# Latent attention's query and key tiles filled straight from the bank, with a new order of the work

## The chip, the cores and the metric

One core of a Trainium2 chip runs the whole kernel. The metric is device time in microseconds (us) for one execution. The engines are TensorE (PE; its weight loads are PEld), VectorE (DVE), ScalarE (ACT), GpSimd (POOL) and SyncE (SP). Transfers are issued by SP, POOL and ACT, each with its own queue. Matmuls read SBUF tiles (`s`, `raw`, `wh`, `wl`) and write PSUM banks (`b`).

## The reference

Two layers run over 256 latent tokens and 256 context tokens of 1024 columns, in float32. Each layer has three attention branches on one projection, then a gated merge, and a squared-ReLU MLP. The branch that matters here is latent attention (`ml`): eight heads whose queries and keys are 64 plain columns and 32 rotated ones; the rotated key is shared by all heads.

```python
q_nope, q_rope = ml_q[..., :MLA_NOPE], ml_q[..., MLA_NOPE:]      # 64 and 32 per head
k_nope = (c_kv @ w_uk).reshape(b, n, MLA_HEADS, MLA_NOPE)
k_rope = ml_kr[:, :, None, :]
...
ml_q = jnp.concatenate([q_nope, q_rope], axis=-1)
ml_k = jnp.concatenate([k_nope, jnp.broadcast_to(k_rope, (b, n, MLA_HEADS, MLA_ROPE))], axis=-1)
...
yc = sdpa_blocks(pl['ml_q'][:, :, :, None, :], mk_all, mv_all, sc_m)
```

Layer 0 computes queries for latent and context tokens (512), layer 1 for the latent ones only (256). Keys always cover 512 tokens.

## The kernel before

Most matmuls are done in three passes: each operand is split into a high part (ScalarE rounds it) and a low part (VectorE subtracts), and `mm3` (L762 to L764) adds high by high, high by low and low by high. `hilo` (L804 to L812) makes such a split of a PSUM bank: ScalarE at L808 or, with a scale, L811; VectorE at L809 or L812. Weights come by SP's queue (L681) and are split at L699 (ScalarE) and L700 (VectorE).

The instructions of each engine stand in one fixed order. A planner in Python makes it before the kernel is built: a list of work items for each layer, written by hand in `SEQ`, gives the order in which items are started, and the planner plays them on modelled engines. In `SEQ`, `c0` to `c7` are the eight chunks of the first norm's modulation (each reads two weight tiles and ends in the L835 and L845 matmuls), `q`, `k`, `v` are neighbourhood attention's projections, `rope` the rotated columns, `l0` to `l3` latent attention's head pairs, `attn` starts the attention units, `g`, `o` and `w` are gates, output projections and modulation weights. A word such as `more4`, `raw1` or `less` changes how much is in flight.

For each pair of heads, `it_ml` computes a bank of 128 rows of plain query columns (64 rows for each head) and a bank of keys, and forks `ml_evac` on each. `ml_evac` takes two tiles, `s0` and `s1`, of 128 rows with a high and a low half:

- `hilo`, called at L1403, splits all 128 rows of the bank into `s0`, one ScalarE and one VectorE operation.
- L1405, a transfer on POOL's queue, copies rows 64 to 127 of `s0` (the second head) to rows 0 to 63 of `s1`.
- L1407, a transfer, puts the second head's 32 rotated rows into rows 64 to 95 of `s1`.
- L1409, a transfer, puts the first head's 32 rotated rows into rows 64 to 95 of `s0`. These rows are what L1405 reads, so L1409 waits until L1405 has landed.

`scores` then runs `mm3` on 96 rows of both tiles (L762, with the form 96*128). Eight pairs in two layers, queries and keys, make 16 calls of `ml_evac`.

Of the kernel before, what the change touches and what calls it, by code (L numbers as in the profile page):

```python
# [10 lines left out]
F32 = mybir.dt.float32  # L11
F32R = mybir.dt.float32r
AF = mybir.ActivationFunctionType
ALU = mybir.AluOpType
# [23 lines left out]
ROWS = (slice(0, 64), slice(64, 128))  # L38
# [27 lines left out]

BR = {"N": NA, "L": ML, "G": GA}
SEQ = (
# [7 lines left out]
)  # L76


# [183 lines left out]
SL_W, SL_E, SL_G = 0.5, 10.0, 13.0  # L262
# [247 lines left out]
def a_(n):  # L510

    return 0.07 + n * 0.00085


def v_(n):
    return 0.07 + n * 0.00104
# [28 lines left out]
class Prog:  # L545
# [852 lines left out]

    def ml_evac(self, l, key, bank, m, scale, rope, mem):

        nc = self.nc
        s0, s1 = self.take(mem), self.take(mem)
        yield from self.hilo(s0.ap[:, 0, :m], s0.ap[:, 1, :m], bank.ap[:, :m], m, scale, SL_E)  # L1403
        self.unbank(bank)
        yield ("pool", 1.2, lambda: nc.gpsimd.dma_start(s1.ap[0:64, :, :m], s0.ap[64:128, :, :m]))  # L1405
        yield from self.wait("qr", l)
        yield ("pool", 1.2, lambda: nc.gpsimd.dma_start(s1.ap[64:96, :, :m], rope(1)))  # L1407
        yield ("sleep", 2.5)
        yield ("pool", 1.2, lambda: nc.gpsimd.dma_start(s0.ap[64:96, :, :m], rope(0)))  # L1409
        yield ("sleep", 3.0)  # L1410
        self.qr_leaf.done()
        self.qr_leaf.done()
        self.qk[key] = [s0, s1]
        self.set(*key)


# [97 lines left out]
    def scores(self, l, br, p, s):  # L1514

        mm = self.nc.tensor.matmul
        if br == ML:
            q, k = (self.qk[(n, l, p)][s].ap[0:96] for n in ("mlq", "mlk"))
            return lambda out, i, j: self.mm3(out, (q[:, 0, i], q[:, 1, i]), (k[:, 0, j], k[:, 1, j]), True, True)
        kq, kk = self.unit_needs(l, br, p)[0]  # L1520
        q, (k, kl) = self.stacked[kq][s], self.stacked[kk]

        def make(out, i, j):
            mm(out, q[:, i], k[s][:, j], start=True, stop=False)  # L1524
            mm(out, q[:, i], kl[s][:, j], start=False, stop=True)  # L1525
        return make
# [645 lines left out]
```

## Time and profile before

| what | value |
| --- | --- |
| device time, median of 3 runs | 1448.34 us (1448.06 to 1448.86) |
| the profiled execution's own time | 1452.61 us |
| its span, first to last instruction | 1450.8 us (1.8 us lie around it) |
| mean granted TensorE clock | 0.991 |
| busy: PE, PEld | 1418.5 us (98%), 1290.5 us (89%) |
| busy: DVE, ACT, POOL | 1081.8 us (75%), 746.6 us (51%), 34.7 us (2%) |
| chain that ended last, by engine | PE 86%, DVE 6%, DMA 4%, ACT 2% |
| transfers | 210.91 MB, mean 145 GB/s |

All times below are those of the profiled execution, counted from the start of its span. The granted clock is in shares of full speed. An engine's idle time matters where the work that ends last waits for it; PE is on that chain for most of the span.

### The profile page before, as it was taken

The numbers are of one execution on the slowest core, as the hardware profiler recorded it, in microseconds if no ns is written. First come the engines' busy times: TensorE is split into PE (matmuls) and PEld (weight loads), VectorE is DVE, ScalarE is ACT, GpSimd is POOL, SyncE is SP. The second block draws the span as 40 slices with busy tenths as digits, with TensorE's granted clock in tenths as the row PEclk, the third lists the DMA queues.
The fourth block names the chain that finished last, engine by engine and source line by source line (L and its number), as shares of the span: only waits on it lengthen the run. The fifth ranks groups of instructions, "written<-read, shape, count | busy, mean of one in ns | idle before, by whom it ended". The sixth has DMA issues, their size and how long they took to land.

```text
span 1450.8 us, 23974 instructions
## 1 busy us (share of the span) xinstructions
PE 1418.5 (98%) x9294; PEld 1290.5 (89%) x9294; DVE 1081.8 (75%) x2251; ACT 746.6 (51%) x1359; POOL 34.7 (2%) x74
## 2 busy tenths in 40 slices
PE   5999999999999999999999999999999999999997
PEld 3799889988888899888888889999998999899997
DVE  6638887859986989888866547758888987766665
ACT  4528876446852344323233244348776874645543
POOL 0000110000000000000000000000111000000000
PEclk9999999999999999999999999999999999999999
DMA  8511433342225544455655424335465436455551
GB/s 324 195 41 56 111 101 90 105 152 78 86 104 189 174 145 132 153 194 180 199 199 193 149 98 141 131 99 160 127 176 144 134 105 219 155 180 188 175 189 45
DMA packets 61779, 210.91 MB, mean 145 GB/s; under 512 B 7392, under 2 KB 9440, under 8 KB 61664
## 3 DMA queue, kind: packets, MB, share of 16 engines
q1 hardware_dynamic: 56448, 197.94, 41.0%
q0 software_dynamic: 4352, 10.49, 3.2%
q8 instruction: 73, 1.20, 0.3%
q10 hardware_dynamic: 864, 0.93, 0.2%
q14 instruction: 42, 0.34, 0.1%
HBM read 200.95 MB, written 1.05 MB: 139 GB/s over the span
## 4 chain that ended last, share of the span: by engine, by line
PE 86%; DVE 6%; DMA 4%; ACT 2%; issue 1%; POOL 0%; ACTq 0%; SPq 0%; DVEq 0%; POOLq 0%
PE b L763 25%; PE b L762 25%; PE b L764 25%; PE b L1696 3%; DMA raw<-in_wts_dram 3%; PE b L1731 2%; PE b L1730 2%; DVE wl L700 1%; PE b L1524 1%; PE b L1525 1%; DMA s<-s 1%; DVE s L905 1%; DVE s L1044 1%; DMA s<-in_wts_dram 1%; PE b L1700 1%
## 5 line engine op out<-in xcount | busy, mean ns | idle before, releaser
L762 PE MATMUL b<-s,wh 128*128 128x256 f32 (+1 forms) x1664 | 566.5, 340 | 1.2 <-ACT s L1047 1.1
L763 PE MATMUL b<-s,wh 128*128 128x256 f32 (+1 forms) x1664 | 561.4, 337 | 0.9 <-DVE s L1905 0.3
L764 PE MATMUL b<-s,wl 128*128 128x256 f32 (+1 forms) x1664 | 559.8, 336 | 0.0
L699 ACT CAST wh<-raw 128x1024 fp32r<-128x1024 f32 (+3 forms) x184 | 188.4, 1027 | 341.8 <-PE b L763 290.1
L762 PEld LDWEIGHTS b<-s,wh 128*128 128x128 f32 x1664 | 317.7, 191 | 34.0 <-ACT s L1047 1.4
L763 PEld LDWEIGHTS b<-s,wh 128*128 128x128 f32 x1664 | 317.8, 191 | 33.3 <-DVE s L1048 1.7
L764 PEld LDWEIGHTS b<-s,wl 128*128 128x128 f32 x1664 | 317.4, 191 | 32.5
L700 DVE TENSOR_TENSOR wl<-raw,wh 128x1024 fp32r<-128x1024 f32 (+3 forms) x184 | 218.8, 1191 | 103.9 <-ACT wh L699 100.1
L905 DVE CUSTOM_DVE_ANT_0 s<-raw,s 128x512 f32<-128x512 f32 x248 | 170.6, 688 | 35.1 <-DMA raw<-in_wts_dram 30.8
L762 PE MATMUL b<-s,s 128*128 128x256 f32 (+4 forms) x568 | 169.5, 298 | 3.1 <-DMA s<-s 3.1
L763 PE MATMUL b<-s,s 128*128 128x256 f32 (+4 forms) x568 | 167.8, 295 | 0.0
L764 PE MATMUL b<-s,s 128*128 128x256 f32 (+4 forms) x568 | 167.5, 295 | 0.0
L762 PEld LDWEIGHTS b<-s,s 128*128 128x128 f32 (+1 forms) x568 | 109.0, 192 | 4.8 <-issue 3.3
L764 PEld LDWEIGHTS b<-s,s 128*128 128x128 f32 (+1 forms) x568 | 109.0, 192 | 2.5
L763 PEld LDWEIGHTS b<-s,s 128*128 128x128 f32 (+1 forms) x568 | 109.2, 192 | 1.4
L809 DVE TENSOR_TENSOR s<-b,s 128x512 fp32r<-128x512 f32 (+3 forms) x151 | 100.1, 670 | 13.1 <-ACT s L808 12.1
L762 PE MATMUL b<-wh,s 128*128 128x256 f32 (+1 forms) x360 | 104.0, 289 | 0.0
L764 PE MATMUL b<-wh,s 128*128 128x256 f32 (+1 forms) x360 | 102.1, 284 | 0.0
L763 PE MATMUL b<-wl,s 128*128 128x256 f32 (+1 forms) x360 | 102.1, 284 | 0.0
L1860 DVE SCALAR_TENSOR_TENSOR s<-b,mod,s 128x256 f32<-128x256 f32 x120 | 55.5, 480 | 60.6 <-PE b L764 60.4
L808 ACT CAST s<-b 128x512 fp32r<-128x512 f32 (+2 forms) x151 | 85.0, 577 | 22.1 <-PE b L764 9.1
L699 ACT CAST wh<-s 128x1024 fp32r<-128x1024 f32 x45 | 47.2, 1049 | 67.9 <-PE b L763 59.0
(157 smaller groups left out, 1892.7 us busy)
## 6 DMA issues: line engine op xcount, KB each, us to landing
raw<-in_wts_dram SPq DMA_DIRECT2D x299, 512.0 KB, 3.5
s<-in_wts_dram SPq DMA_DIRECT2D x61, 512.0 KB, 3.6
s<-in_xT_dram SPq DMA_DIRECT2D x16, 256.0 KB, 6.2
s<-s POOLq DMA_DIRECT2D x28, 128.0 KB, 4.2
s<-in_bias_dram POOLq DMA_DIRECT2D x16, 192.0 KB, 2.7
s<-s POOLq DMA_DIRECT2D x12, 256.0 KB, 3.7
raw<-in_wts_dram SPq DMA_DIRECT2D x4, 384.0 KB, 3.0
raw<-in_wts_dram SPq DMA_DIRECT2D x3, 432.0 KB, 3.8
```

What stands on the lines that cost most here:

```text
L699: yield from self.act(n, lambda: nc.scalar.copy(hi[:, :n], r[0][:, :n]), SL_W)
L700: yield from self.dve(n, lambda: nc.vector.tensor_tensor(lo[:, :n], r[0][:, :n], hi[:, :n].bitcast(F32), ALU.subtract), SL_W)
L762: mm(out, a[0], b[0], start=start, stop=False)
L763: mm(out, a[0], b[1], start=False, stop=False)
L764: mm(out, a[1], b[0], start=False, stop=stop)
L808: yield from self.act(n, lambda: nc.scalar.copy(hi, src), slack)
L809: yield from self.dve(n, lambda: nc.vector.tensor_tensor(lo, src, hi.bitcast(F32), ALU.subtract), slack)
L905: yield ("dve", 0.73, lambda: nc.vector.tensor_tensor_reduce(self.junk, w[0][:, r], self.crow[j][:, r], 1.0, 0.0, ALU.mult, ALU.add, accum ...
L1696: nc.tensor.transpose(ps[:, c * P:(c + 1) * P], pt[:, c * P:(c + 1) * P], self.ident)
L1730: mm(ps, v[o + k], hi[:, k, :], start=k == 0, stop=False)
L1731: mm(ps, v[o + k], lo[:, k, :], start=False, stop=k == nk - 1)
L1860: yield from self.dve(NLAT, lambda: nc.vector.scalar_tensor_tensor(o, bank.ap[:, i * NLAT:(i + 1) * NLAT], g[:, c, j:j + 1], x, ALU.mult, ...
```

## The change

`ml_evac` takes two tiles, one for each head, and uses all 128 rows of them. Each head's 64 rows stay in the rows that they have in the bank, so the first head's tile has the plain part in rows 0 to 63, the rotated part in rows 64 to 95 and zeros in 96 to 127; the second head's has zeros in rows 0 to 31, the rotated part in 32 to 63 and the plain part in 64 to 127. ScalarE and VectorE each do two operations of 64 rows in place of one of 128. GpSimd fills the zero rows. The 64-row transfer is gone, both transfers of rotated rows remain, and the scores contract over 128 rows. `SEQ` is rewritten for both layers; only the first line of each is shown.

```diff
 SEQ = (
-    "start c2 k0 c4 c0 q1 c6 c1 k1 k2 raw2 c7 c3 yL more4 q0 rope less c5 v1 v0 q3 ckv w attn yN q2 l1 k3 l0 l3 "
...
+    "start more4 yL c2 v1 c7 c0 c3 c4 c1 raw2 k1 c6 c5 k2 q1 w rope q0 q3 less v0 k0 ckv q2 attn yN l1 k3 l0 gG7 "
...
     def ml_evac(self, l, key, bank, m, scale, rope, mem):
-        nc = self.nc
-        s0, s1 = self.take(mem), self.take(mem)
-        yield from self.hilo(s0.ap[:, 0, :m], s0.ap[:, 1, :m], bank.ap[:, :m], m, scale, SL_E)
+        nc = self.nc
+        t = [self.take(mem), self.take(mem)]
+        zero, rot = (slice(96, 128), slice(0, 32)), (slice(64, 96), slice(32, 64))
+        def hi():
+            for s in range(2):
+                o, x = t[s].ap[ROWS[s], 0, :m], bank.ap[ROWS[s], :m]
+                if scale is None:
+                    nc.scalar.copy(o, x)
+                else:
+                    nc.scalar.activation(o, x, AF.Copy, scale=scale)
+        def lo():
+            for s in range(2):
+                h, x = t[s].ap[ROWS[s], 0, :m].bitcast(F32), bank.ap[ROWS[s], :m]
+                o = t[s].ap[ROWS[s], 1, :m]
+                if scale is None:
+                    nc.vector.tensor_tensor(o, x, h, ALU.subtract)
+                else:
+                    nc.vector.scalar_tensor_tensor(o, x, scale, h, ALU.mult, ALU.subtract)
+        for s in range(2):
+            yield ("pool", 1.2, lambda: nc.gpsimd.memset(t[s].ap[zero[s], :, :m].bitcast(F32), 0.0))
+        yield ("act", 2 * a_(m), hi, SL_E)
+        yield ("dve", 2 * v_(m), lo, SL_E)
         self.unbank(bank)
-        yield ("pool", 1.2, lambda: nc.gpsimd.dma_start(s1.ap[0:64, :, :m], s0.ap[64:128, :, :m]))
         yield from self.wait("qr", l)
-        yield ("pool", 1.2, lambda: nc.gpsimd.dma_start(s1.ap[64:96, :, :m], rope(1)))
-        yield ("sleep", 2.5)
-        yield ("pool", 1.2, lambda: nc.gpsimd.dma_start(s0.ap[64:96, :, :m], rope(0)))
-        yield ("sleep", 3.0)
+        for s in range(2):
+            yield ("pool", 0.6, lambda: nc.gpsimd.dma_start(t[s].ap[rot[s], :, :m], rope(s)))
+        yield ("sleep", 5.0)
         self.qr_leaf.done()
         self.qr_leaf.done()
-        self.qk[key] = [s0, s1]
+        self.qk[key] = t
         self.set(*key)
...
-            q, k = (self.qk[(n, l, p)][s].ap[0:96] for n in ("mlq", "mlk"))
+            q, k = (self.qk[(n, l, p)][s].ap for n in ("mlq", "mlk"))
```

The change moves instructions. On POOL, the place of layer 1's third head pair in before (queries 2x256, keys 1024; `s_7707` and `s_7708` are the rotated rows of queries and keys):

```order
L1405 DMA s_9258<-s_9257 64x2x256 [waits DMASW5_49,DMASW4_49,DVE_49]
L1407 DMA s_9258<-s_7707 32x2x256
L1405 DMA s_9389<-s_9259 64x1024 [waits DMASW2_49,DVE_49]
L1407 DMA s_9389<-s_7708 32x1024 [waits DMASW7_49]
L1409 DMA s_9257<-s_7707 32x2x256 [waits DMASW4_49]
L1409 DMA s_9259<-s_7708 32x1024 [waits DMASW6_49,DMASW1_49]
```

The same place in the changed kernel (`s_9302` and `s_9303` are the two query tiles, `s_9304` and `s_9435` the key tiles; the rotated rows are `s_7727` and `s_7728`):

```order
L1423 MEMSET s_9302 32x2x256 [waits DVE_49,PE_49,DMASW1_49,Activation_49,Pool_49]
L1423 MEMSET s_9303 32x2x256 [waits DMASW2_49,DVE_49,Pool_49]
L1423 MEMSET s_9304 32x1024 [waits DVE_49,DMASW3_49,Activation_49,Pool_49]
L1423 MEMSET s_9435 32x1024 [waits DVE_49,DMASW4_49,PE_49,Pool_49]
L1429 DMA s_9302<-s_7727 32x2x256 [waits DMASW0_49]
L1429 DMA s_9303<-s_7727 32x2x256
L1429 DMA s_9304<-s_7728 32x1024
L1429 DMA s_9435<-s_7728 32x1024
```

In before all but the second row wait, for VectorE (`DVE_49`) or for an earlier transfer (`DMASW`), the last two for the landing of the 64-row copies; in the changed order the fills come first, behind the former users of their tiles, and then the four transfers of rotated rows, of which only the first waits, for a transfer.

On PE, at the program's start, the last matmuls ahead of chunk 5 in before (`s_113` to `s_120` are the eight chunks of 128 model columns, `s_118` is chunk 5; `wh` and `wl` are halves of weights):

```order
L762 MATMUL b_75<-s_117,wh_73 128x512
L763 MATMUL b_75<-s_117,wh_73 128x512
L764 MATMUL b_75<-s_117,wl_74 128x512
L762 MATMUL b_77<-s_113,s_134 128x512
L763 MATMUL b_77<-s_113,s_134 128x512
L764 MATMUL b_77<-s_113,s_135 128x512
L762 MATMUL b_77<-s_114,s_134 128x512
L763 MATMUL b_77<-s_114,s_134 128x512
L764 MATMUL b_77<-s_114,s_135 128x512
L762 MATMUL b_82<-s_118,wh_69 128x512 [waits Activation_49]
L763 MATMUL b_82<-s_118,wh_69 128x512 [waits DVE_49]
```

And in the changed kernel:

```order
L762 MATMUL b_77<-s_117,wh_73 128x512
L763 MATMUL b_77<-s_117,wh_73 128x512
L764 MATMUL b_77<-s_117,wl_74 128x512
L762 MATMUL b_79<-s_113,s_121 128x512 [waits Activation_49]
L763 MATMUL b_79<-s_113,s_121 128x512
L764 MATMUL b_79<-s_113,s_124 128x512 [waits DVE_49]
L762 MATMUL b_79<-s_114,s_121 128x512
L763 MATMUL b_79<-s_114,s_121 128x512
L764 MATMUL b_79<-s_114,s_124 128x512
L762 MATMUL b_76<-wh_71,s_118 128x256 [waits Activation_49]
L763 MATMUL b_76<-wl_72,s_118 128x256
L764 MATMUL b_76<-wh_71,s_118 128x256 [waits DVE_49]
```

In before, chunk 5 is first read after 17 groups of three matmuls of 512 columns; in the changed order after 7 of 512 and 5 of 256 columns.

## Rows read from the trace of the kernel before

**Rows 1.** The page, busy time, share of the span and instructions of each engine.
```profile
PE 1418.5 (98%) x9294; PEld 1290.5 (89%) x9294; DVE 1081.8 (75%) x2251; ACT 746.6 (51%) x1359; POOL 34.7 (2%) x74
```

**Rows 2.** PE's waits: engine, line, releaser, total us, times, longest us.
```profile
PE b L835 <- DMA raw<-in_wts_dram: 13.7, 4, 12.1
PE b L762 <- DMA s<-s: 3.1, 1, 3.1
```

**Rows 3.** Timeline of PE, 1095 to 1106: start, length, line, operation, [idle before <-releaser].
```profile
1095.53 0.28 PE L764 MATMUL b<-s,wl 128*128 128x256 f32 x1
1098.96 0.77 PE L762 MATMUL b<-s,s 96*128 96x512 f32 x1 [3.15 <-DMA s<-s]
...
1105.39 0.28 PE L762 MATMUL b<-s,wh 128*128 128x256 f32 x1
```

**Rows 4.** Windows: length, busy of PE, PEld, DVE, ACT, POOL, PEclk, DMA share, GB/s.
```profile
1095.00:1100.00 5.00, 1.85 (x10) 1.48 (x10) 2.42 (x7) 1.44 (x2) 0.32 (x1) 0.84 1.15 258
1100.00:1105.00 5.00, 5.00 (x19) 4.50 (x18) 3.11 (x6) 2.78 (x6) 1.03 (x2) 0.50 0.42 105
1110.00:1115.00 5.00, 5.00 (x39) 4.76 (x38) 5.00 (x10) 4.43 (x10) 0.00 (x0) 1.00 0.35 119
```

**Rows 5.** The critical chain, 1080 to 1100: start us, length us, what.
```profile
1084.61 0.54 POOL s L1407
...
1085.22 6.92 DMA s<-s
...
1092.68 6.14 DMA s<-s
```

**Rows 6.** Groups by form, ScalarE and VectorE: busy us, mean ns.
```profile
L1158 ACT ACTIVATE s<-b 64x512 fp32r<-64x512 f32 x8 | 4.7, 592 | 0.1
...
L811 ACT ACTIVATE s<-b 128x512 fp32r<-128x512 f32 x6 | 3.6, 592 | 2.5 <-PE b L1356 2.5
...
L811 ACT ACTIVATE s<-b 128x256 fp32r<-128x256 f32 x6 | 2.3, 380 | 5.3 <-PE b L1356 3.6 <-PE b L764 1.7
...
L1166 DVE SCALAR_TENSOR_TENSOR s<-b,s 64x512 fp32r<-64x512 f32 x8 | 5.5, 689 | 2.1 <-ACT s L1158 1.9
...
L812 DVE SCALAR_TENSOR_TENSOR s<-b,s 128x512 fp32r<-128x512 f32 x6 | 4.1, 685 | 2.1 <-ACT s L811 2.0
...
L812 DVE SCALAR_TENSOR_TENSOR s<-b,s 128x256 fp32r<-128x256 f32 x6 | 2.5, 420 | 1.7 <-ACT s L811 1.7
```

**Rows 7.** Groups by line and form, PE.
```profile
L762 PE MATMUL b<-s,wh 128*128 128x512 f32 x816 | 322.5, 395 | 0.1
...
L762 PE MATMUL b<-s,s 96*128 96x512 f32 x32 | 14.0, 437 | 3.1 <-DMA s<-s 3.1
```

**Rows 8.** Groups by line and form, POOL.
```profile
L1071 POOL MEMSET s<- 128x256 f32 x1 | 0.3, 307 | 0.0
...
masks.py:197 POOL MEMSET ident<- 128x128 f32 x1 | 0.2, 204 | 0.3 <-POOLq L2160 0.3
```

**Rows 9.** Windows of layer 0's attention, columns as in rows 4.
```profile
100.00:150.00 50.00, 49.70 (x340) 45.60 (x340) 38.54 (x111) 36.52 (x81) 2.14 (x4) 1.00 0.16 49
150.00:200.00 50.00, 50.00 (x298) 43.92 (x297) 42.63 (x110) 41.38 (x95) 9.57 (x19) 1.00 0.50 132
350.00:400.00 50.00, 49.88 (x303) 42.82 (x302) 47.18 (x104) 42.07 (x100) 0.00 (x0) 1.00 0.22 76
```

**Rows 10.** The start: window, then timelines of SyncE and PE.
```profile
0.00:50.00 50.00, 33.25 (x229) 22.29 (x230) 30.44 (x66) 21.34 (x35) 1.22 (x10) 0.93 0.89 322
...
33.00 0.33 SPq L681 DMA_DIRECT2D s<-in_wts_dram  x1
34.73 0.33 SPq L681 DMA_DIRECT2D raw<-in_wts_dram  x1
...
37.77 0.64 PE L835 MATMUL b<-s,s 128*32 128x256 f32 x8 [0.40 <-DMA s<-in_wts_dram]
...
51.57 0.40 PE L762 MATMUL b<-s,wh 128*128 128x512 f32 x1
```

12 rows, old and new, of the table SEQ are left out of this document.

## The prediction

> **What bounds the kernel now.** I read the page's busy shares first. TensorE (PE) is busy for 98% of the span [rows 1]; the other engines have slack. So the time can fall only where PE stands still or runs at a lower clock, or where its work shrinks. The wait list shows where it stands still [rows 2]: 13.7 us for weight tiles at L835, nearly all of it one wait at the program's start, and then one wait of 3.1 us at L762 for a transfer from one SBUF tile to another. That is the longest single wait outside the start, and it belongs to the code that the change rewrites.
>
> The timeline places it [rows 3]: the last matmul before it starts at 1095.53, the first one of latent attention's third head pair in layer 1 at 1098.96, after 3.15 us of waiting. The stall costs more than its length. The windows [rows 4] give a granted clock of 0.84 in the 5 us with the stall and 0.50 in the next 5, where 19 matmuls run; from 1110 on, at 1.00, 39 do. In the timeline full pace is back at 1105.39. So some 6.4 us (1098.96 to 1105.39) ran at half speed, which wastes another 3.2 us. **The whole price of the stall is 3.15 + 3.2 = 6.3 us.**
>
> The chain of waits says what was late [rows 5]: two transfers in series. The 64-row copy of the second head (L1405) was issued at 1085.22 and took 6.92 us; only then could L1409 overwrite its source with rotated rows, issued at 1092.68, landing 6.14 us later. The window around it has a DMA share of 1.15 [rows 4], so other transfers shared the DMA engines; these two took 6 to 7 us each.
>
> **The change, part by part.**
>
> *The 64-row transfers and their series.* Sixteen L1405 transfers go, and with them the wait of L1409 for their landing. In the order of before, 100 PE rows, about 12.6 us of PE work, stand between the last matmul into the key bank of layer 1's third pair and its first score. The two landings alone, 6.92 + 6.14, are 13.1 us, and with evacuation and issue ahead they did not fit. In the changed order 102 PE rows, about 12.9 us, stand there, and the path from the bank is two ScalarE and two VectorE operations on 64x512, by [rows 6] 2 x 0.59 + 2 x 0.69 = 2.6 us (the longer ones of those rows). Slack is some 10 us. What is late next is the rotated rows: POOL issues them behind four zero fills. The latest PE instruction that those fills wait for stands some 27 us of PE work ahead of the first score; four fills of at most 0.93 us (below), four issues of 0.54 us [rows 5] and the slower landing, 6.92 us, make 12.8 us. That fits twice. The other seven pairs did not stall before, and in the new order none is nearer. **I take the full 6.3 us; the bounds are 0 (the rotated rows still come late) and 6.3.**
>
> *128 rows instead of 96 in the scores.* The matmul count is the same. A 96-row matmul of 512 columns takes 437 ns in the mean, with the half-clock ones among them, a 128-row one 395 [rows 7]; rows of the contraction cost nothing here. Zero.
>
> *Two operations of 64 rows instead of one of 128.* Sixteen more on ScalarE and sixteen more on VectorE. A 64-row operation lasts as long as a 128-row one: 592 against 592 ns on ScalarE, 689 against 685 on VectorE [rows 6]. So the change adds 12 x 0.59 + 4 x 0.38 = 8.6 us of ScalarE and 12 x 0.69 + 4 x 0.42 = 10.0 us of VectorE work; in layer 0 alone, 8 of each on 512 columns, 4.7 and 5.5 us. Cover: VectorE works 81 of the 100 us from 100 to 200, and 64 of the 80 from 100 to 180 if the second row is spread evenly [rows 9]. But the new table of order also packs that stretch. Multiplying the instructions of each order by their mean durations, I get 14% more VectorE work than before in the 80 us of PE work from 100 on, so about 73 of 80 us, 91% in place of 80%. Before shows that PE bears this: from 350 to 400 VectorE is busy for 47.18 of 50 us and PE for 49.88 [rows 9]. I charge 1 us for small waits, with bounds of 0 and 8 (rivals).
>
> *32 zero fills on GpSimd.* They aren't in the trace. Two fills there take 204 ns for 128 and 307 for 256 columns [rows 8], 0.8 ns a column: an estimate of 0.93 us for 1024 columns and 0.51 for 512, 24 x 0.93 + 8 x 0.51 = 26 us on an engine that is busy for 34.7 of 1450.8 us. Nothing waits behind them but the rotated rows. Zero; the other bound is that each fill holds VectorE up for its length, 16 x 0.93 = 15 us in layer 0.
>
> [...]
>
> *The table of order at the start.* Chunk 5 of the model's eight column chunks is the last that the projections get; in the changed order its two modulation tiles stand five places earlier in SyncE's queue. That looks like several us, since its first matmul ran at 51.57 [rows 10], and the start as a whole costs 50 - 33.25 = 16.75 us [rows 10]. But PE had other work to fill that time: from 37.77 on it hardly waited. Before it did 17 groups of three matmuls (0.69 us each, 11.7 us) ahead of chunk 5; the changed order has 7 such groups and 5 of 256 columns (0.36 us), 6.6 us. So after must reach chunk 5 at 51.57 - (11.7 - 6.6) = 46.5 to break even. In before, the tile in the place where chunk 5's second one now stands was issued at 34.73; the one ahead of it was issued at 33.00 and used on landing at 37.77, 4.8 us later [rows 10], so I put this one's landing at 39.6. Then L835 0.6, 5.9 us of other groups and 0.4 of L845 lead to 46.6. **Break-even; I take a gain of 0.5 us**, bounds -2 and +3 (the tile comes earlier because buffers come free earlier).
>
> *Other moves by the table.* In layer 0's second norm the matmul that sums squares (L967) comes 1.4 us of PE work behind the last projection matmul, 2.1 before. That is 0.7 us less cover for the squares that it needs; I charge 0.5 us, with bounds of 0 and 0.7. From layer 1's second norm on the PE order is the same, so the waits there stay.
>
> **Sum.** -6.3 - 0.5 + 1.0 + 0.5 = -5.3 us. The profiled execution took 1452.61 us, 1450.8 of it span; it would take 1447.3. The median of the runs is 1448.34, 4.3 below the profiled one, and I take the same difference off it: **1443.0 us**.
>
> **The rivals.**
>
> *A: as summed, 1443.0* (1439 to 1446 by the start and the small waits). For it: every step of the stall is in the trace, and the slack is 10 us. Chance 0.62.
>
> *B: the stall goes, but new small waits eat most of it.* The new table moves every wait; each short one may drop the clock as in [rows 4]. Two new waits of 1 us with as much lost at half clock are 4 us: 1447. Chance 0.16, half of it within 0.2%.
>
> *C, the other side: VectorE becomes the bound in layer 0's attention.* Place: 100 to 180. It decides from the point where VectorE's work passes the 80 us of PE work, that is, if my 91% is 10% too low. At 5% over, PE stands 4 us and loses as much again at half clock, with the start at -2: 1443 + 8 + 2 = 1453. Against it: the 350 to 400 window. Chance 0.08.
>
> *D: the change doesn't do what it says.* The rotated rows, queued on POOL behind fills that wait for buffers, are as late as the copy was. Then 1443.0 + 6.3 = 1449.3. Against it: 27 us of lead against 12.8. Chance 0.08.
>
> *E: fills hold VectorE up.* 15 us of blocking on some 7 us that the packed stretch has free would cost PE 8 us and up to as much again at half clock: 1451 to 1459. Against it: the fills are short and come at most four in a row, with transfers between them. Chance 0.06. [...]
>
> **How the numbers follow.** A measurement of this kernel tells 0.2%, 2.9 us, from no change: faster means below 1445.4, slower above 1451.2. A gives 0.57 faster and 0.05 same; B 0.08 and 0.08; D 0.07 same and 0.01 slower; C 0.08 slower; E 0.05 slower and 0.01 same. Together faster 0.65, same 0.21, slower 0.14. The range leaves out C, E and the outermost gain of the start, 0.18 in all: 1438.5 (A with 3 us more from the start and 1.5 less in small waits) to 1449.5 (D).
>
> **What would show it.** Right: no wait of PE for an SBUF-to-SBUF transfer, and a clock of 1.00 where layer 1's attention runs; L1429 issued well ahead of the scores; 64-row operations at 0.59 and 0.69 us; fills below 1 us with VectorE's mean durations unchanged; chunk 5 near 46.5. Wrong: PE waits for VectorE or ScalarE between 100 and 200, a wait of L762 for L1429 or L1423, VectorE operations that grow beside fills, or a chunk 5 more than 2 us from 46.5.

## The result, and the profile after

The changed kernel is slower: 1456.9 us median (1454.28 to 1457.48, 4 runs) against 1448.6 us (1448.06 to 1449.66), a ratio of 1.005 with a 95% interval of 1.0034 to 1.0066. Forecast were 1443.0 us and a range that ended at 1449.5. Measured once more beside other kernels it took 1456.61 us against 1449.6, ratio 1.0039 (1.0027 to 1.005). So the change costs 7 to 8 us where 5 were to be won. One profiled execution ran disturbed, that of e9 (1550.22 us at a mean granted clock of 0.847); it is set beside nothing here.

The profiled execution took 1457.28 us. The page's row of busy shares, to be held against [rows 1], and then PE's waits, to be held against [rows 2] (engine, line, releaser, total us, times, longest us):

```profile
PE 1428.8 (98%) x9294; PEld 1292.1 (89%) x9294; DVE 1091.1 (75%) x2267; ACT 756.3 (52%) x1375; POOL 53.7 (4%) x90
```

```profile
PE b L835 <- DMA raw<-in_wts_dram: 11.6, 2, 11.2
PE b L1716 <- ACT s L1696: 1.5, 2, 1.1
PE b L969 <- ACT s L945: 1.2, 1, 1.2
...
PE b L1544 <- DVE s L1760: 0.9, 1, 0.9
...
PE b L1544 <- DVE s L1164: 0.4, 1, 0.4
```

The wait for a transfer between SBUF tiles is gone. New are small waits of the softmax's transposes (L1716, the L1696 of before) and of the other branches' scores (L1544) for ScalarE and VectorE. PE is busy for 10 us more with the same number of matmuls: some of them run at half pace (matmuls of 512 columns 0.43 us from start to start in place of 0.23), as the start will show.

The groups by form (busy us, mean ns | idle before), to be held against [rows 6, 8]:

```profile
L1412 ACT ACTIVATE s<-b 64x512 fp32r<-64x512 f32 x8 | 4.7, 586 | 0.1
...
L1421 DVE SCALAR_TENSOR_TENSOR s<-b,s 64x512 fp32r<-64x512 f32 x8 | 5.5, 683 | 0.2
...
L1423 POOL MEMSET s<- 32x1024 f32 x24 | 23.1, 964 | 37.2 <-PE b L1545 15.0 <-PE b L1751 13.0 <-ACT s L808 4.2
```

The durations are those of the sum: 0.59, 0.68 and 0.96 us. The windows, with the columns of [rows 4, 9], the first to be held against the window in [rows 10]:

```profile
0.00:50.00 50.00, 38.38 (x219) 24.75 (x220) 31.13 (x67) 22.03 (x36) 1.23 (x10) 1.00 0.86 309
100.00:150.00 50.00, 49.13 (x336) 44.98 (x335) 31.26 (x91) 32.77 (x71) 4.94 (x7) 1.00 0.22 69
150.00:200.00 50.00, 49.78 (x296) 42.09 (x295) 47.50 (x123) 44.11 (x100) 17.95 (x26) 1.00 0.33 93
...
1095.00:1100.00 5.00, 5.00 (x38) 4.74 (x37) 4.13 (x7) 4.90 (x7) 0.00 (x0) 1.00 0.52 133
1100.00:1105.00 5.00, 5.00 (x39) 4.80 (x38) 4.78 (x12) 4.97 (x10) 0.00 (x0) 1.00 0.67 222
```

Where PE stood and then ran at a clock of 0.50 before, it now does 38 and 39 matmuls in 5 us at 1.00. None of the new waits in the attention stages shows in the granted clock: it reads 1.00 in every 50 us from 100 to 250 and from 1050 to 1200. From 150 to 200 VectorE is busy for 47.5 us in place of 42.6. The timelines of POOL and of PE show layer 1's third pair: the last fills, the four transfers of rotated rows, and the pair's first score, 48 us later and without a wait.

```profile
1051.19 2.41 POOL L1423 MEMSET s<- 32x1024 f32 x3 [8.40 <-PE b L1751]
1053.57 2.05 POOL L1429 DMA_DIRECT2D s<-s  x4
...
1103.86 0.40 PE L762 MATMUL b<-s,s 128*128 128x512 f32 x1
```

Three landmarks divide the executions. They are the first L986 matmul of layer 1's first norm, that of its second norm, and the end of the span. The same PE work lies ahead of each in every kernel here, apart from the experiments' own edits, and the norm rows come from the timeline of PE. Where two kernels have the same matmuls on PE in the same order, their starts can also be compared one by one; such differences, "counted from chunk 5" below, are taken from the first matmul on chunk 5 on, so that the start is left out of them.

| profiled execution | to layer 1's first norm | from there to its second | span |
| --- | --- | --- | --- |
| before, the one of the rows ahead | 894.62 | 356.90 | 1450.8 |
| before, a second one (e1) | 896.15 | 352.07 | 1447.2 |
| changed | 902.09 | 354.09 | 1455.5 |
| changed, a second one (e13) | 897.50 | 354.30 | 1450.7 |

Read alone, the first row and the third say that layer 1 won 2.8 us and that layer 0 and the start lost 7.5. The second executions say otherwise: in layer 1 before varies by 4.8 us, up to layer 1's first norm the changed kernel by 4.6.

### The profile page after: what moved, and what is told of

Its sections match the earlier page's. It is cut to its first block, busy times and chain, and to the rows that moved or that the text cites. A ratio compares the mean times of both kernels' runs of the same rounds, so it can differ in the third digit from the quotient of the medians.

```text
span 1455.5 us, 24040 instructions
## 1 busy us (share of the span) xinstructions
PE 1428.8 (98%) x9294; PEld 1292.1 (89%) x9294; DVE 1091.1 (75%) x2267; ACT 756.3 (52%) x1375; POOL 53.7 (4%) x90
## 4 chain that ended last, share of the span: by engine, by line
PE 83%; DVE 8%; ACT 4%; DMA 3%; issue 1%; ACTq 0%; SPq 0%; DVEq 0%
PE b L763 24%; PE b L762 24%; PE b L764 24%; DMA raw<-in_wts_dram 3%; PE b L1716 2%; PE b L1751 2%; DVE wl L700 2%; PE b L1750 2%; ACT s L1687 1%; PE b L1544 1%; DVE s L809 1%; PE b L1545 1%; PE b L835 1%; ACT wh L699 1%; DVE s L905 1%
## 5 line engine op out<-in xcount | busy, mean ns | idle before, releaser
L762 PE MATMUL b<-s,wh 128*128 128x512 f32 (+1 forms) x1664 | 567.0, 341 | 1.2 <-ACT s L1047 1.1
L763 PE MATMUL b<-s,wh 128*128 128x512 f32 (+1 forms) x1664 | 561.5, 337 | 0.7 <-DVE s L1925 0.3
L764 PE MATMUL b<-s,wl 128*128 128x512 f32 (+1 forms) x1664 | 559.8, 336 | 0.0
L699 ACT CAST wh<-raw 128x1024 fp32r<-128x1024 f32 (+2 forms) x183 | 187.7, 1028 | 327.3 <-PE b L763 261.5
L700 DVE TENSOR_TENSOR wl<-raw,wh 128x1024 fp32r<-128x1024 f32 (+2 forms) x183 | 218.1, 1194 | 105.0 <-ACT wh L699 100.6
L905 DVE CUSTOM_DVE_ANT_0 s<-raw,s 128x512 f32<-128x512 f32 x236 | 162.3, 688 | 39.8 <-DMA raw<-in_wts_dram 36.2
L762 PE MATMUL b<-s,s 128*128 128x256 f32 (+2 forms) x584 | 172.8, 296 | 0.0
L763 PE MATMUL b<-s,s 128*128 128x256 f32 (+2 forms) x584 | 171.1, 293 | 0.0
L764 PE MATMUL b<-s,s 128*128 128x256 f32 (+2 forms) x584 | 171.1, 293 | 0.0
L764 PEld LDWEIGHTS b<-s,s 128*128 128x128 f32 x584 | 112.1, 192 | 2.0
L763 PEld LDWEIGHTS b<-s,s 128*128 128x128 f32 x584 | 112.2, 192 | 1.4
L762 PEld LDWEIGHTS b<-s,s 128*128 128x128 f32 x584 | 112.1, 192 | 1.5
L809 DVE TENSOR_TENSOR s<-b,s 128x512 fp32r<-128x512 f32 (+1 forms) x143 | 94.7, 671 | 18.9 <-ACT s L808 18.2
L808 ACT CAST s<-b 128x512 fp32r<-128x512 f32 (+1 forms) x143 | 80.5, 578 | 30.7 <-PE b L764 15.5
L699 ACT CAST wh<-s 128x1024 fp32r<-128x1024 f32 (+1 forms) x46 | 47.8, 1040 | 72.0 <-PE b L763 54.4
```

The lines of the kernel that those rows point to most:

```text
L699: yield from self.act(n, lambda: nc.scalar.copy(hi[:, :n], r[0][:, :n]), SL_W)
L700: yield from self.dve(n, lambda: nc.vector.tensor_tensor(lo[:, :n], r[0][:, :n], hi[:, :n].bitcast(F32), ALU.subtract), SL_W)
L762: mm(out, a[0], b[0], start=start, stop=False)
L763: mm(out, a[0], b[1], start=False, stop=False)
L764: mm(out, a[1], b[0], start=False, stop=stop)
L808: yield from self.act(n, lambda: nc.scalar.copy(hi, src), slack)
```

## The experiments

The theory drawn from this profile was that the time goes to three places: the start, where PE runs at half pace for longer; the added operations and fills in the attention stages; and a stall that is smaller in most executions than in the one profiled. The rivals were that the new table of order alone carries the loss, or that the new filling alone does. "Before", run beside each of them, took 1449.27 to 1449.91 us.

| kernel | median us (runs) | ratio to before, 95% interval |
| --- | --- | --- |
| e1, before again | 1449.41 (10) | 0.9998 (0.9986 to 1.0009) |
| e2, new filling, old table | 1462.3 (4) | 1.0087 (1.0067 to 1.0107) |
| e3, old filling, new table | 1460.41 (5) | 1.0075 (1.0056 to 1.0093) |
| e4, changed, old words up to attn in layer 0 | 1455.29 (10) | 1.004 (1.0029 to 1.005) |
| e5, changed, no added operations | 1452.49 (12) | 1.0022 (1.001 to 1.0033) |
| e6, before with the added operations | 1460.52 (6) | 1.0076 (1.0061 to 1.0092) |
| e7, changed, fills twice | 1460.31 (6) | 1.0076 (1.0061 to 1.0091) |
| e8, layer 0 as before, layer 1 as changed | 1451.34 (12) | 1.0011 (1.0002 to 1.002) |
| e9, before, new filling for one pair | 1455.57 (4) | 1.0039 (1.0026 to 1.0052) |
| e10, changed, no fills | 1459.32 (5) | 1.0066 (1.0053 to 1.0079) |
| e11, changed, no fills, no added operations | 1449.74 (11) | 1.0001 (0.9991 to 1.0011) |
| e12, before, dense matmuls at the start | 1452.36 (12) | 1.0019 (1.0009 to 1.0029) |
| e13, changed again | 1456.61 (12) | 1.0039 (1.0027 to 1.005) |
| e14, changed, no added VectorE operations | 1453.92 (12) | 1.0023 (1.0013 to 1.0033) |
| e15, changed, half the fills | 1457.26 (6) | 1.0046 (1.0032 to 1.0059) |
| e16, e9 again | 1456.22 (7) | 1.0039 (1.0026 to 1.0052) |

**e1: before again.** No edit.

> The kernel before, unchanged, profiled a second time. If the 3.15 us stall of the third head pair in layer 1 belongs to every execution, the second profile shows it again at 3 to 3.5 us with about 6 us at half clock behind it, and the profiled time is some 4 us above the median again. If it belongs to the first profiled execution alone (transfers slowed there), the second shows under 1.5 us, and its time is nearer to 1448.6.

The profiled execution took 1449.02 us, near the median. Its waits, timeline and windows at the same place:

```profile
PE b L762 <- DMA s<-s: 1.0, 1, 1.0
```

```profile
1097.21 0.28 PE L764 MATMUL b<-s,wl 128*128 128x256 f32 x1
1098.44 0.47 PE L762 MATMUL b<-s,s 96*128 96x512 f32 x1 [0.96 <-DMA s<-s]
```

```profile
1100.00:1105.00 5.00, 5.00 (x39) 4.74 (x38) 5.00 (x12) 4.52 (x11) 0.49 (x1) 1.00 0.76 173
```

The chain of waits has the same two transfers in series:

```profile
1086.90 5.44 DMA s<-s
...
1092.87 5.44 DMA s<-s
```

They took 5.44 us each in place of 6.92 and 6.14. A wait of 0.96 us, and behind it 39 matmuls in 5 us at 1.00: no half clock. The wait is real, its price in this execution is 1 us. Counted from chunk 5, the two executions of before stay within 1 us of each other up to the stall, the one that the forecast used loses 5.0 us on e1 across it, and behind it the two keep their distance within 0.7 us. So the stall is what set the profiled execution 4.3 us above its median.

**e2 and e3: filling and table apart.** e2 is the changed kernel with before's table, e3 before with the new table (the tables are abbreviated here):

```diff
-SEQ = (new table)
+SEQ = (old table)      # e2
...
-SEQ = (old table)
+SEQ = (new table)      # e3, with ml_evac and scores of before
```

> New filling of the tiles and 128-row scores, old table of order in both layers. As the prediction has it (stall 6.3 us in every execution, the added operations free): 1442 to 1443.5. If the stall is not in most executions of before: 1447 to 1449. If the added 64-row operations or the zero fills stall PE in layer 0 (VectorE full): 1451 or more, with waits of PE for ScalarE or VectorE between 100 and 200 us.

> Old filling with its 64-row transfers, new table of order in both layers. Theory that the table costs time at the start (PE at half pace until 47.6 us instead of 33.7): 4 us slower there, 1452 to 1457, whatever the filling does. Rival, that the added operations cost the time and the table is harmless: 1446 to 1449.

Both halves alone are worse than both together, by 5.7 us (e2) and 3.8 us (e3) against e13. The new filling in the old table costs 13 us, of which the profiles of e2 and e1 show 2.8 at the start; so the added work isn't hidden there; e2's waits name the softmax:

```profile
PE b L1716 <- ACT s L1696: 4.0, 2, 3.2
...
PE b L1716 <- DVE s L1698: 2.0, 2, 1.8
...
PE b L1750 <- ACT s L1687: 1.5, 1, 1.5
```

e3 keeps transfers that PE waits for (2.1 us in two waits) and has a wait of 3.2 us for ScalarE in layer 1. Each table suits its own filling; neither theory as stated holds.

**e4: the start in the old order.** In layer 0's row of the table the words up to `attn` are put in the order of before (with `q2` moved ahead of `attn`).

```diff
-    "start more4 yL c2 v1 c7 c0 c3 c4 c1 raw2 k1 c6 c5 k2 q1 w rope q0 q3 less v0 k0 ckv q2 attn ...
+    "start c2 k0 c4 c0 q1 c6 c1 k1 k2 raw2 c7 c3 yL more4 q0 rope less c5 v1 v0 q3 ckv w q2 attn ...
```

> The changed kernel with the words of layer 0 up to attn in the order of before, all else new. Theory of the start (half pace of PE until 47.6): the full pace comes near 33.7 again and 4 us of the changed kernel's time go, 1452 to 1453.5. Rival, that the loss sits in layer 0's attention (VectorE at 95% from 150 to 200): 1456 to 1458, unchanged within 1 us.

1455.29 us, 1.3 under e13 (below); their intervals overlap, so this is not told from nothing. In its profile full pace came for good at 44.7 us, not near 33.7. The order of the first words alone doesn't bring it early.

**e5, e14 and e6: the added operations.** e5 is the changed kernel in the same order on every engine, without the second operations; e14 takes only VectorE's away:

```diff
-            for s in range(2):
+            for s in range(1):      # in hi() and lo() (e5), in lo() alone (e14)
...
-        zero, rot = (slice(96, 128), slice(0, 32)), ...
+        zero, rot = (slice(96, 128), slice(0, 128)), ...
```

> The changed kernel in the very same order on every engine, without the 16 added ScalarE and 16 added VectorE operations: the second head's tile is filled with zeros by the same GpSimd fill (128 rows in place of 32), so the second head's plain query and key rows are left out of the result. Theory that the added 64-row operations make PE wait in the attention stages: 3 to 5 us under the changed kernel, 1452 to 1453.5, with no wait of PE over 0.5 us between 100 and 250. Rival, that order, fills or the start cost the time: 1456 to 1457.

> The changed kernel in the same order with the added ScalarE operations but without the 16 added VectorE ones (the second head's low parts are zeros, so its products with low parts are left out of the result). If VectorE, the busiest engine beside PE, carries the cost of the added operations: near 1452.5, as without both. If ScalarE does: near 1456.5. If both share it: 1454 to 1455.

e5 is 4.1 us under e13, e14 2.7. By that VectorE's added operations (10 us of its time) cost PE about 2.7 us and ScalarE's about 1.4, but the intervals of e5 and e14 overlap, so the split is rough. The traces show where the time goes. Counted from chunk 5, e5 gains 1.5 us on e13 in layer 0's attention, in steps of some 0.2 us and less, and 2.4 us in layer 1's. More than half of the latter, 1.4 us, falls at one matmul, a transpose of the softmax; e14 gains the same there. Timeline of VectorE, ScalarE and PE, first e13, then e5:

```profile
1062.87 1.38 DVE L1419 TENSOR_TENSOR s<-b,s 64x512 fp32r<-64x512 f32 x2
1064.28 1.23 DVE L700 TENSOR_TENSOR wl<-raw,wh 128x1024 fp32r<-128x1024 f32 x1
1065.43 0.22 DVE L1699 RECIPROCAL sm<-sm 128x1 f32<-128x1 f32 x2
1065.62 0.72 ACT L1696 ACTIVATE s<-s,sm 128x512 f32<-128x512 f32 x1 [1.61 <-DVE sm L1699]
1066.39 1.09 PE L1716 MATMUL b<-ident,s 128*128 128x128 f32 x8 [1.22 <-ACT s L1696]
```

```profile
1061.68 0.67 DVE L1419 TENSOR_TENSOR s<-b,s 64x512 fp32r<-64x512 f32 x1
...
1065.15 1.03 PE L1716 MATMUL b<-ident,s 128*128 128x128 f32 x8
```

In e13 VectorE has no gap over 0.1 us from 1058.7 to 1065.6. In that stretch stand both doubled subtractions (L1421, on 64x256, and L1419), ahead of the reciprocal that ScalarE, and through it PE, waits for. The stretch starts late, too: ahead of it VectorE waits 1.72 us for a weight tile. In the five profiles where this wait for the tile lasts 1.6 to 1.9 us and the added VectorE operations are there (changed, e7, e10, e13, e15), PE waits 1.0 to 1.4 us. Without them (e5, e11, e14) VectorE waits 0.6 to 1.2 us for the tile and PE not at all; e4 has the operations but no wait for the tile, and PE has none either. In these profiles it takes both. Whether the added operations are what makes the tile late in the five, no run here shows.

e6 puts the same additions into before, in the same order on every engine, by splitting rows 64 to 127 of the bank a second time:

```diff
+        rows = (slice(0, 128), slice(64, 128))
...
+            for r in rows:
+                nc.scalar.activation(s0.ap[r, 0, :m], bank.ap[r, :m], AF.Copy, scale=scale)
```

> The kernel before in the very same order, transfers and all, with one more ScalarE and one more VectorE operation of 64 rows behind each of the 16 fillings (the second half of the bank is split twice, into the same place). Theory of the added operations: 3 to 8 us slower than before, 1452 to 1457, through waits of PE for ScalarE or VectorE in both attention stages and a later 64-row transfer in layer 1. Rival, that they are hidden: 1449 to 1450.5.

There they cost 11 us, more than they last on either engine. In the profiles, counted from chunk 5, e6 loses 5.2 us on e1 in layer 0's attention, wins 1.0 back up to layer 1's first norm and loses 5.7 from there to the second, 9.9 in all; the start adds 2.7. Part is in new waits:

```profile
PE b L1713 <- DVE s L1695: 4.3, 5, 2.3
...
PE b L1748 <- DVE s L809: 1.0, 3, 0.5
```

L1713 and L1695 are the softmax's transposes and the scaling of its rows (L1696 and L1678 of before). From layer 1's first norm to its second e6 takes 357.77 us, 5.7 more than e1.

**e7, e15 and e10: the fills.** e7 does each fill twice; e15 scores first heads on 96 rows and fills only second heads' tiles; e10 has no fills.

```diff
-    ... lambda: nc.gpsimd.memset(t[s].ap[zero[s], :, :m].bitcast(F32), 0.0)
+    ... lambda: [nc.gpsimd.memset(t[s].ap[zero[s], :, :m].bitcast(F32), 0.0) for _ in range(2)]    # e7
+    ... lambda: s and nc.gpsimd.memset(t[s].ap[zero[s], :, :m].bitcast(F32), 0.0)                  # e15
+    ... lambda: None                                                                           # e10
...
-    ... self.qk[(n, l, p)][s].ap ...
+    ... self.qk[(n, l, p)][s].ap[0:128 if s else 96] ...                      # e15
+    ... self.qk[(n, l, p)][s].ap[slice(64, 128) if s else slice(0, 96)] ...     # e10
```

> The changed kernel with every zero fill done twice, all else in the same order. If the fills hold VectorE up (one tensor_scalar of 256 columns lasted 1.13 us beside a fill, where 0.35 is usual): 1 to 4 us slower, 1458 to 1461, and more such long operations. If the fills are hidden: 1456 to 1457.5.

> The changed kernel with first heads scored on rows 0 to 95, as in before, so that only second heads' tiles are filled: 16 fills in place of 32, the result complete. If fills cost 2.7 us: 1455 to 1456, half of it gone. If they cost nothing: as e13_change_again within 0.7 us.

> The changed kernel in the same order without the 32 zero fills: first heads are scored on 96 rows, second heads on their 64 plain rows alone (their rotated rows are left out of the result; their transfers are still made). Doubling the fills cost 3.4 us; if the first set costs as much: 1452.5 to 1455, and no tensor_scalar of VectorE over 0.5 us. If only the second set hurt: 1456 to 1457.

Doubling costs about 3.7 us against e13, halving wins nothing (1457.26 against 1456.61, the intervals overlap). Counted from chunk 5, e7 loses 3.8 us on e13 in layer 0's attention and nothing more in layer 1's; the waits that it adds there are for VectorE:

```profile
PE b L1751 <- DVE s L809: 1.5, 2, 0.8
...
PE b L1720 <- DVE s L809: 0.8, 1, 0.8
PE b L1720 <- DVE s L1698: 0.6, 1, 0.6
```

e10 came out 2.7 us slower than e13, for which it has a cause of its own: PE's first matmul of a score on 64 rows took longer, 488 ns in the mean against 417 on 96 rows.

```profile
L762 PE MATMUL b<-s,s 64*128 64x512 f32 x16 | 7.8, 488 | 0.0
L762 PE MATMUL b<-s,s 96*128 96x512 f32 x16 | 6.7, 417 | 0.0
```

With those of 256 columns (331 ns against 305) these rows make 1.3 us, some half of the 2.7; the rest is not explained. So e10 doesn't tell what the fills cost. A longer VectorE operation beside a fill is seen in the scaling of the softmax's rows, one tensor_scalar for each (durations in ns, least, median, greatest; first and last start). In the changed kernel, in e7 and in e10:

```profile
L1698 DVE TENSOR_SCALAR s<-s,sm x90: 324/477/1130, 123.7 to 1190.2; 128x512 f32<-128x512 f32 x56, 128x256 f32<-128x256 f32 x34
```

```profile
L1698 DVE TENSOR_SCALAR s<-s,sm x90: 324/477/1322, 123.3 to 1193.5; 128x512 f32<-128x512 f32 x56, 128x256 f32<-128x256 f32 x34
```

```profile
L1698 DVE TENSOR_SCALAR s<-s,sm x90: 326/477/489, 122.8 to 1193.2; 128x512 f32<-128x512 f32 x56, 128x256 f32<-128x256 f32 x34
```

Of these 90, four last over 0.5 us in the changed kernel (up to 1.13), 13 in e7 (up to 1.32) and one in e15, which has half the fills. In e10 and e11, without fills, none lasts over 0.49, nor in the two executions of before (0.491). The timeline of the changed kernel has the fill beside the long one:

```profile
172.20 1.39 DVE L1698 TENSOR_SCALAR s<-s,sm 128x256 f32<-128x256 f32 x2
172.43 1.02 POOL L1423 MEMSET s<- 32x1024 f32 x1
```

One of these two lasts the 1.13 us of the list, 0.8 us more than the least of its kind (0.32), with a fill running beside it. The subtractions don't show this: four fills run from 166.26 to 170.21, and the two of L1419 at 166.75 last 1.38 us together, 0.69 each, where the mean of all sixteen is 0.685. With one set of fills 4 of the 90 are long, and the price is small: e15 is 0.7 us under e13 at the end of layer 0's attention, counted from chunk 5, and that is gone again by layer 1.

**e11: neither fills nor added operations.** e10's and e5's edits, with both heads scored on the first head's tile.

```diff
+            for s in range(1):
...
+    ... lambda: None
...
+    ... self.qk[(n, l, p)][0].ap[slice(0, 96)] ...
```

> The changed kernel in the same order without fills and without the added operations: both heads of a pair are scored on the first head's tile (the second head's queries and keys are left out of the result). What is left is the new table of order and the missing 64-row transfers. If added operations (4.4 us) and fills (3 us) are the whole loss and the stall's 1 to 3 us are won: 1447 to 1450. If the new table costs by itself, at the start or in layer 0: 1452 or more.

1449.74 us, as before. The new table without the 64-row transfers gains nothing: 351.04 us in layer 1, 1.0 under e1, about what e1's stall cost, and 1.2 us more than e1 up to layer 1's first norm. In its profile it is 1.3 us under e5 from chunk 5 to layer 1's second norm; the 2.7 between the medians is not all seen there.

**e8, e9 and e16: the change in part.** e8 has before's filling and table in layer 0 and the new ones in layer 1. e9 has before's table and the new filling for layer 1's third pair alone.

```diff
+        if l == 0:                   # e8, with (old SEQ[0], new SEQ[1])
+        if key[1:] != (1, 2):        # e9, e16, with the old SEQ
+            yield from self.ml_evac_copy(l, key, bank, m, scale, rope, mem)
+            return
```

> Layer 0 with the old filling and the old order, layer 1 with the new filling and the new order. In the traces layer 1 from its first norm to its second takes 352.7 us in the changed kernel, 355.5 and 350.7 in two executions of before. Theory that layer 0 and the start carry the loss: 1447 to 1451, no difference from before that can be measured. Rival, that layer 1's new order carries 3 us or more of it: 1452 or more.

> The kernel before and its old order, with the new filling and 128-row scores for layer 1's third head pair alone, where the 64-row transfer was waited for; the planner moves a few instructions behind it. If the stall is all that the change could win: 1445 to 1448.5, that wait gone. If the added operations (two on ScalarE, two on VectorE, four fills) delay the softmax of the pairs ahead of it by as much: 1449 to 1452.

> The kernel before with the new filling for layer 1's third head pair alone, once more for its profile. It was 6 us slower than before with four added operations and four fills. If new waits carry that, PE's waits for ScalarE or VectorE from 1000 to 1200 grow by 3 us or more. If its start carries it, full pace for good comes after 44 us again, where before had it by 36.

e8 is 1.9 us slower than before: layer 1's part of the change loses a little instead of winning 6.3. e16 repeats e9 for its profile. It has the third pair's wait for the transfer gone, full pace for good by 34.6, and 356.16 us from norm to norm, 4.1 more than e1. The timelines of POOL and of PE show where:

```profile
1104.67 0.49 POOL L1409 DMA_DIRECT2D s<-s  x1 [1.07 <-DMA s<-s]
1110.21 0.47 PE L762 MATMUL b<-s,s 96*128 96x512 f32 x1 [1.06 <-ACT wh L699]
```

```profile
1150.75 0.66 PE L1736 MATMUL b<-ident,s 128*128 128x128 f32 x4 [0.86 <-DVE s L1718]
1151.74 0.50 PE L1564 MATMUL b<-s,s 128*128 128x512 f32 x1 [0.34 <-ACT s L1707]
```

The row at 1110.21 is the first score of the fourth pair, whose tiles are still filled as in before. The view names ScalarE's weight split, which that score doesn't read. PE's queue stood there for transfers, too, and the trace has the fourth pair's L1409, issued at 1104.67 behind that pair's 64-row transfer, landing at 1110.08. So the stall moved from the third pair to the fourth, and waits for softmax steps came some 40 to 50 us behind that. The four operations more on ScalarE and VectorE win nothing.

**e12: dense work at the start.** Two matmuls on weight tiles behind each of the eight modulation chunks of layer 0; in the profile each stands as two rows, 32 in all.

```diff
+                if l == 0 and h == 1:
+                    for _ in range(2):
+                        nc.tensor.matmul(ps[:, 260:512], w[0][:, 0:P], w[0][:, 260:512], start=True, stop=True)
```

> The kernel before with two matmuls of 128x252 on weight tiles, written to unused columns, behind each of layer 0's eight modulation chunks at the start: work that PE has to do more, while it waits for tiles or runs at half pace. If the start is bound by PE's half pace and dense work brings the full pace sooner: 1444 to 1448, full pace for good by 30 us. If it is bound by the tiles' arrival, or PE's pace doesn't rise: 1449 to 1456.

1452.36 us, 2.5 slower. In its profile (1451.01 us) PE kept full pace nearly throughout from 21.2 us on (eight L835 matmuls last 0.64 us at 26.7, 1.08 at 16.2), earlier than in any other profile here (33 us and later); one profile doesn't prove that the dense work brought it. The 32 added rows keep PE busy for some 10 us themselves (6.5 and 3.4 us in the groups by form); that this is more than the pace gives back is my reading of the sum.

**e13: the changed kernel again.** No edit.

> The changed kernel, unchanged, measured beside the next three. By the sum of parts (before 1449.5, new table and missing transfers 0, fills 2.7, added operations 4.4): 1456 to 1457.5. If its first measurement was off: more than 2 us from that.

As expected in the median. Its runs fall in two groups (time, mean granted clock of each run):

```
1452.51 0.991   1452.58 0.992   1453.04 0.994   1453.60 0.992   1454.70 0.996   1456.56 0.991
1456.67 0.996   1457.22 0.996   1457.34 0.997   1457.65 0.996   1457.92 0.996   1458.79 0.988
```

The profiled execution is the first of them, 4.8 us faster than the one of the result. The difference lies in the start. Timeline of PE, first the changed kernel as in the result, then e13:

```profile
39.23 0.63 PE L764 MATMUL b<-s,wl 128*128 128x512 f32 x1
...
47.16 0.63 PE L764 MATMUL b<-s,wl 128*128 128x512 f32 x1
...
48.18 0.39 PE L764 MATMUL b<-s,wl 128*128 128x512 f32 x1
...
50.45 0.28 PE L762 MATMUL b<-wh,s 128*128 128x256 f32 x1
```

```profile
38.46 0.63 PE L763 MATMUL b<-s,wh 128*128 128x512 f32 x1
38.89 0.53 PE L764 MATMUL b<-s,wl 128*128 128x512 f32 x1
...
42.45 0.39 PE L763 MATMUL b<-s,wh 128*128 128x512 f32 x1
...
46.31 0.28 PE L762 MATMUL b<-wh,s 128*128 128x256 f32 x1
```

The last row of each is the first matmul on chunk 5. Up to there the two executions do the same work in the same order; in the first PE's matmuls of 512 columns last 0.63 us (0.43 from start to start) until 47.6 and then 0.39 (0.23), in the second the pace changes at 38.9, from 0.63 to 0.39 us, and chunk 5 comes 4.1 us earlier. From there to the end of the span the two differ by 0.6 us, so nearly all of the 4.8 us is the start. Executions with before's words at the start came to full pace for good at 33.1, 35.6 (e1), 35.2 (e8) and 34.6 us (e16), but at 46.2 (e2), 45.8 (e6) and 44.7 (e4) too; those with the new words at 38.9 (e13), 40.0 (e5) and 40.2 (e11), or at 45.6 to 48.0 (changed, e3, e7, e10, e14, e15). As the pace differed between two executions of one and the same program, full from 47.6 in one and from 38.9 in the other, I take this as a toss with odds: 4 of 7 against 3 of 9 early ones. The four early ones with before's words (the first profile, e1, e8, e16) are those whose layer 0 is before's throughout; the runs here don't tell whether that is chance.

## Why the prediction was wrong

- **The step that failed first: "The whole price of the stall is 3.15 + 3.2 = 6.3 us", and then "I take the same difference off it".** Both numbers were read rightly, but from one execution that stood 4.3 us above its median. In e1 the same wait took 0.96 us and no half clock followed; across the stall alone the two executions part by 5.0 us. By e11 against e1, what is to be won in layer 1 is 1.0 us. The difference between profile and median was in the text and was carried through the sum as a constant; it was the stall. The forecast took it off both as an offset and as a gain.
- **Mechanism of the change, right.** The transfer's wait is gone, the rotated rows go out long before they are needed, 64-row operations last 0.59 and 0.68 us, fills 0.96 us (0.93 estimated), and e15, which scores half of the heads on 96 rows, is no faster than the 128 rows of e13. The 0.5 us charged at layer 0's second norm did not show: the changed kernel's waits list has none for it.
- **The term "I charge 1 us for small waits" was mis-sized, and the cover behind it was worked out for layer 0 alone.** The added operations cost 4.1 us by the medians of e5 and e13; in their traces, counted from chunk 5, 1.5 in layer 0's attention and 2.4 in layer 1's. In layer 0 VectorE came out as packed as forecast, 91% over 80 us, and PE stayed busy for 79 of them, as this window of e13 shows (columns as in [rows 4]); the one wait of 0.9 us in it, at L1544, is in e5 and e11 too, so it comes with the new table.

```profile
120.00:200.00 80.00, 78.96 (x483) 67.83 (x482) 73.10 (x197) 69.05 (x158) 22.46 (x32) 1.00 0.30 85
```

  In layer 1, for which no cover was worked out, VectorE had no gap for 7 us, behind a late weight tile and with the added operations ahead of a step of the softmax that PE needed. The means over 50 and 80 us hid that stretch. The row that was to show that PE bears it (350 to 400) shows a stage where the work is spread otherwise.
- **The fills, "Zero".** Between 0 (e15) and some 3 us (e5 to e11 is 2.7 by the medians and 1.3 by the traces, but e11 changes the scores too). The runs don't settle it. What rival E is named for is there, in the softmax's tensor_scalars: up to 1.13 us beside fills where the least is 0.32, small in all with one set of fills and 3.7 us with two (e7).
- **The start, "Break-even".** Chunk 5 at 46.5 was right for e13 (46.31) and 4 us early for the profiled execution (50.45): the working took PE's pace as full from 38 on and had no term for the pace. By the runs of e13 this is worth about 4 us when it goes badly, and it went badly in 6 of 9 profiles with the new words. Whether those odds belong to the new words, seven and nine profiles don't settle.
- **Rivals.** B had the form (stall gone, small waits) but only to 1447, and the half clock that it charged behind each did not come; C had the side and the engine, but named layer 0's attention, where PE bore most of it. Together, from e1 to e13: 1.4 us up to layer 1's first norm, although e13 came to chunk 5 at its best, and 2.2 us from there to the second norm, 3.5 in the span; the rest of the 7 us between the medians is the start's toss, as far as the groups of e13 show.

## What to carry to other kernels

A stall read from one execution may be that execution's alone; where the profile stands 4 us above the runs, look for the difference in the profile's own stalls before taking it off as a constant. Work added to an engine with slack in the mean was not free here, where its steps form a chain between two matmuls: 1.3 us more on two engines together at 512 columns (0.59 and 0.68), 0.8 at 256, in 16 places, cost 4 us in a table of order made for it, and 11 us in one that was not. Two executions with the same order of matmuls can be compared matmul by matmul, which tells a start that differs from work that costs. And an order that is written out by hand belongs to its code: filling and table exchanged singly were each worse than either kernel.

## What the runs showed of the hardware

- With one and the same program, the changed kernel, PE's matmuls of 512 columns came from 0.63 down to 0.39 us for good at 38.9 us in one execution (e13) and at 47.6 in another (the one of the result). The first matmul on chunk 5 came 4.1 us later in the second (50.45 against 46.31).
- The column of the granted clock did not show it: in the changed kernel it reads 1.00 from 0 to 50 us, while matmuls of 512 columns last 0.63 us until 47.2 and 0.39 from 48.2. Here the durations told what the column did not.
- A score on 64 rows cost PE a mean of 488 ns for its first matmul, on 96 rows 417 (e10); the second and third on 64 rows last 393 and 389 ns. In the timeline of e10 a first matmul on 64 rows and 256 columns lasts 0.38 us behind one on 128 rows (204.95) or on 96 (219.68), and 0.28 behind a score on 64 (205.41, 220.14). That the change of the row count makes it longer is my reading of these rows; it wasn't tried by itself.
- In the changed kernel, beside a GpSimd fill of 1.02 us, a VectorE tensor_scalar lasted 1.13 us, 0.8 longer than the least of its kind (0.32), while the subtractions of 512 columns that read PSUM kept a mean of 0.68 us. With the fills doubled 13 of 90 tensor_scalars lasted over 0.5 us in place of 4, without fills none (e10, e11).
- Two transfers between SBUF tiles, in series, took 6.92 and 6.14 us in one execution of before and 5.44 us each in another. PE waited 3.15 us for them in the first, and its granted clock fell to 0.50 behind the wait; it waited 0.96 us in the second, and the clock stayed at 1.00.
